# The two meta rows of a mixer output: matmuls replaced by elementwise products and a sum over partitions

## The chip, the cores and the metric

The kernel runs on one core of one Trainium2 chip. The metric is the device time of one execution, in microseconds (us); the time before is the median of three runs. Below, PE is TensorE, DVE is VectorE, ACT is ScalarE, POOL is GpSimd and SP is SyncE, whose queue issues nearly all DMA transfers.

## The reference

One layer of a hybrid decoder over 1024 tokens of 1024 channels, with 16 learned meta tokens ahead of them. Two mixers (a gated linear recurrence and a multi-scale pooling) give `z`, which is projected, normed and added to the residual; a gated MLP with a causal depthwise convolution of width 3 follows.

```python
z = sigmoid(gate_a) * (a @ w_branch_hgrn) + sigmoid(gate_b) * (p @ w_branch_pool)
h = h + rmsnorm(z @ w_out, mix_norm_post)
u = rmsnorm(h, ffn_norm_pre)
gt = causal_dwconv(u @ ffn_w_gate, ffn_conv_w, ffn_conv_b)      # 3 taps over time
y = (gelu(gt) * (u @ ffn_w_up)) @ ffn_w_down
h = h + rmsnorm(y, ffn_norm_post)
return h[:, N_META:]
```

The output drops the 16 meta tokens. The convolution looks two tokens back, so the MLP needs the residual of the last two meta tokens as well: two rows more than 1024. These two rows (the code calls them the halo, tile 8) are what the change is about: their part of `z @ w_out`.

## The kernel before, in words

All matrix products are done in float32 by splitting each operand into a high part (rounded to the format that TensorE multiplies at full rate, `F32R`) and a low part (the rest). A product then takes three matmuls: high by high, high by low, low by high (`mm3`, lines 245 to 248). High parts are made by casts on ACT, low parts by subtractions on DVE.

The stage around the change is the seam between the mixers and the MLP. `z` lies with its channels on the partitions, as 8 blocks `z[k]` of 128 channels by 1026 tokens; the first two token columns are the halo. `w_out` comes in 8 blocks of 128 channels by 1024 outputs (`wo` k). The 1024 rows are worked in three groups of row tiles of 128: tiles 0, 1, 2; then 3, 4, 5; then 6, 7. For group 0 the blocks k run upwards, for group 1 downwards, for group 2 upwards. A token `k.g.k.t` is one step: block k into tile t of group g, that is 6 matmuls of 512 columns (two halves of the outputs by three parts). Each tile accumulates in a pair of PSUM banks; there are four pairs.

The two halo rows are tile 8 of group 0. In step `k.0.k.8` their 2 columns of high and 2 columns of low z are the stationary operand, next to each other: 4 columns against the high weights and 2 against the low ones, for each half of the outputs, so 4 matmuls of 512 columns in each of the 8 steps (`mix_halo`, line 1453). That leaves high and low results in four rows; `part` copies them to SBUF and moves the low ones by a DMA to the first two partitions, and `join` adds them (lines 1494 to 1501).

Each `wo` k is read from `w_out` into one of three `wraw` buffers (line 1404), cast to `whi` (`wh.k`, line 1408), its rest put into `wlo` (`wl.k`, line 1412), three buffers each. `wl` also stores both parts to DRAM (`wos`, line 1414), because groups 1 and 2 need blocks again whose buffers are gone: `LOADS` says after which step which block is read back (line 1420), and into which buffers. `z[k]` is split for each group separately (`zh.g.k` on ACT, line 1329; `zl.g.k` on DVE, line 1333) into slots of a pool of 26 (`fm`).

When a tile is complete, its row work follows: `ga` (times a gain, line 1511) and `sq` (sum of squares on ACT, line 1506) read the PSUM pair and free it; `ad` adds the residual row (loaded by `res`) and stores the row; `qq`, `no` norm again; `tr` transposes 8 blocks on PE (line 1533); `up`, `lo` write high and low parts of the result as operands of the MLP. Rows 4 to 7 get further steps (`tk`, `su`, `di`, `b22`, `t1` to `t4`, `la`), which make the sums that a Strassen form of the MLP's first two matrices wants. Tokens `P1.e`, `P2.e` are the first products of that form; their weight parts were stored in DRAM earlier as `kept`, and the first of these need the `wraw` buffers.

The order of this stage is written out by hand: the string `SEAM` is a list of tokens, and each engine's instructions keep the order of the tokens (a manual schedule for PE, ACT, DVE and POOL). SP's order is not written out: the scheduler sets it from its own model of time. Waits are placed by the framework from data and buffers.

Of the kernel before, what the change touches and what calls it, by code (L numbers as in the profile page):

```python
# [14 lines left out]
P = 128  # L15
D = 1024
# [51 lines left out]
SEAM = ("k.0.0.0 wh.2 zh.0.4 wl.2 k.0.0.1 zh.0.5 zl.0.4 zh.0.6 k.0.0.2 zl.0.5 zh.0.7 zl.0.6 zh.1.7 k.0.0.8 zl.0.7 "  # L68
# [25 lines left out]
def trunk_kernel(ctx: ExitStack, tc: tile.TileContext, x, meta_tokens, mix_norm_pre,  # L94
# [1222 lines left out]
    def split_z(g, k):  # L1317
        at, n = HALO + GROUPS[g][0] * P, len(GROUPS[g]) * P
        if g == 2:
            if k % 2 == 0:  # L1320
                z_pairs[k // 2] = slot(4 * n, F32R, "zc")
            zc = z_pairs[k // 2][:, (k % 2) * 2 * n : (k % 2 + 1) * 2 * n]
        else:
            zc = slot(2 * n + (0 if g else 2 * HALO), F32R, "zc")
        cuts = [(zc[:, :n], zc[:, zc.shape[1] - n :], z[k][:, at : at + n])]
        if g == 0:
            cuts.append((zc[:, n : n + HALO], zc[:, n + HALO : n + 2 * HALO], z[k][:, :HALO]))
        for hi, _, src in cuts:
            act.copy(hi, src)

        def low():
            for hi, lo, src in cuts:
                dve.tensor_tensor(lo, src, rr(hi), ALU.subtract)

        return cuts[0][0], cuts[0][1], zc[:, n : n + 2 * HALO], low

    zt = ubig(F32, "z").rearrange("p (k t) -> p k t", k=KD)
    z0 = []
    def job_steps(kind, i):
        src, n_k, xs, chunks, post = job(kind, i)  # L1340
        if kind in ("BA", "BB"):
            load_gate(sas if kind == "BA" else sbs, kind == "BB", i)
            if kind == "BA" and i < EARLY_B:
                load_gate(sbs, True, i)
        ws = loader.next()
        if (kind, i) == ("BA", KD - 1):
            for k in range(ZA):
                z0.append(split_z(0, k))
                z0[k][3]()
        spare = [bank("spare") for _ in range(1 if (kind, i) == branch[-1] else 0)]  # L1350
        for b_ in spare:
            act.copy(b_[:, :1], eps_t)
        banks = [bank("p" + kind.lower()) for _ in chunks]
        for k, _ in enumerate(proj_steps(n_k, xs, chunks, ws, banks)):
            if k == 0:
                for b_ in spare:
                    act.copy(b_[:, 1:2], eps_t)
                loader.split()
            if k == n_k // 2 - 1:
                loader.low()  # L1360
                loader.load()
            yield
        if n_k == 1:
            loader.split()
            loader.low()
            loader.load()
        pay()
        after[kind, i] = post(banks)
        if kind == "BB" and i < EARLY_B:
            nc.sync.dma_start(sd[KD + i], sbs[i])  # L1370
        if kind == "BA":
            dve.tensor_tensor(sas[i], sas[i], sbs[i], ALU.add)
            z[i] = sas[i]
# [36 lines left out]
    def wo_low(k):  # L1410
        raw, hi, lo = wo[k]
        dve.tensor_tensor(lo, raw, rr(hi), ALU.subtract)
        for h, t in enumerate((hi, lo)):
            nc.sync.dma_start(wos[k][h], rr(t))
        wo[k] = hi, lo

    def wo_load(k, *tags):
        wo[k] = [slot(D, F32R, "wx") if t == "fm" else wst.tile([P, D], F32R, tag=t, name=nm(t)) for t in tags]
# [19 lines left out]
        z_at[g, k] = split_z(g, k)  # L1438

    def mix_tile(g, k, i, x_):  # L1440
        (whi, wlo), (zh, zl, _, _) = wo[k], z_at[g, k]
        t = slice(i * P, (i + 1) * P)
        ks = z_ks[g]
        for j in range(2):
            n = slice(j * 512, (j + 1) * 512)
            mm3(x_[:, n], (zh[:, t], zl[:, t]), (whi[:, n], wlo[:, n]), k == ks[0], k == ks[-1])

    def mix_halo(k, x_):
        (whi, wlo), (_, _, zm, _) = wo[k], z_at[0, k]
        for j in range(2):  # L1450
            n = slice(j * 512, (j + 1) * 512)
            for c, w in ((2 * HALO, whi), (HALO, wlo))[:: -1 if k else 1]:
                pe.matmul(x_[:c, n], zm[:, :c], w[:, n], start=(k == 0 and c > HALO), stop=(k == KD - 1),
                          skip_group_check=True)
# [21 lines left out]
    class Row:  # L1476
# [11 lines left out]
        def load(self):  # L1488
# [1 line left out]
            self.res = slot(D, name="row2")  # L1490
            nc.sync.dma_start(self.res[: self.n],
                              meta_tokens[T0:NM, :] if i == HALO_ROWS else x[0, i * P : (i + 1) * P, :])

        def part(self):
            both, self.low = slot(D, name="mhl"), slot(D, name="mlow")
            act.copy(both[: 2 * HALO], self.x[: 2 * HALO])
            nc.sync.dma_start(self.low[:HALO], both[HALO : 2 * HALO])
            self.x = both

        def join(self):  # L1500
            dve.tensor_tensor(self.x[:HALO], self.x[:HALO], self.low[:HALO], ALU.add)
# [55 lines left out]
        def last(self):  # L1557
            negdiff(dve, self.t2, self.t2, "b21", self.d)

    STEPS = dict(res=Row.load, part=Row.part, join=Row.join, sq=Row.square, ga=Row.gain, ad=Row.add, qq=Row.square2, no=Row.norm,  # L1560
                 tr=Row.turn, up=Row.up, lo=Row.low1, tk=Row.take, su=Row.sums, di=Row.diff, la=Row.last,
                 b22h=lambda r: upper("b22", r.c22, r.s), b22l=lambda r: lower("b22", r.c22, r.s),
                 t2h=lambda r: upper("t2", r.t2, r.d), t2l=lambda r: lower("t2", r.t2, r.d),
# [150 lines left out]
    for k in range(2):  # L1714
        wo_high(k)
        wo_low(k)
    ffn.lead, ffn.whole_pair = 3, True
    _, off, wide = ffn.span(0)
    x_ffn = {}
    LOADS = {(0, 7): ((4, "fm", "fm"),), (1, 7): ((3, "whi", "wlo"),), (1, 6): ((2, "whi", "wlo"),),  # L1720
             (1, 5): ((1, "whi", "wlo"),), (0, 6): ((0, "wraw", "wraw"),), (2, 0): ((5, "wraw", "wraw"),),
             (2, 1): ((6, "whi", "wlo"),), (2, 2): ((7, "whi", "wlo"),)}

    def seam(token):
        what, *arg = token.split(".")
        arg = [int(a) for a in arg]
        if what == "k":
            g, k, t = arg
            if t not in tiles_:
                tiles_[t] = pair("pm")  # L1730
            if t == HALO_ROWS:
                mix_halo(k, tiles_[t])
            else:
                mix_tile(g, k, t - GROUPS[g][0], tiles_[t])
            if t == (HALO_ROWS if g == 0 else GROUPS[g][-1]):
# [210 lines left out]
```

## Time and profile before

| | |
|---|---|
| median of 3 runs | 1315.32 us (1314.69 to 1315.69) |
| the profiled execution, its own time | 1315.41 us |
| its span, first to last instruction | 1313.4 us |
| mean granted TensorE clock | 0.996 |
| busy: PE, DVE, ACT, POOL | 1296.2, 920.3, 533.1, 362.7 us |
| group 0 of the mixer output, first matmul to the first of group 1 | 558.25 to 599.16 us |
| first matmul of the MLP products | 660.17 us |

A row of the timeline gives start, duration, engine, line of the kernel, operation, output and inputs, shape and count; in brackets the idle time before it and what ended it. A row of the groups gives line, engine, operation, names, shapes and count, then busy time in us and the mean of one in ns, then the idle time before. A row of waits gives who waited for whom: total us, times, the longest. The duration of a matmul in the timeline is from its start to its last result, longer than the distance to the next one.

### The profile page before, as it was taken

The page shows a single profiled execution, that of the slowest core. Times are in us where ns is not written, and L with a number is a line of the kernel's source. Part 1 is how long each engine was busy: PE and PEld are TensorE (multiplying, and loading weights), DVE is VectorE, ACT ScalarE, POOL GpSimd, SP SyncE. Part 2 cuts the span into 40 slices and gives each one's busy share as a digit, 9 for nine tenths or more (in the row PEclk, how much of TensorE's full clock was granted, in tenths as well). Part 3 has the DMA queues.
Part 4 walks back from the last instruction along what each step waited for, and adds up shares of the span by engine and source line. Part 5 has one row for each costly group of instructions (what it writes and reads, how often), then busy time and mean ns, then how long its engine had stood idle before and what let it go on. Part 6 is the DMA issues. An engine that isn't in the chain of part 4 may idle for free.

```text
span 1313.4 us, 19369 instructions
## 1 busy us (share of the span) xinstructions
PE 1296.2 (99%) x7385; PEld 1154.8 (88%) x7385; DVE 920.3 (70%) x1285; ACT 533.1 (41%) x946; POOL 362.7 (28%) x285
## 2 busy tenths in 40 slices
PE   8999999999999999999999999999999999999996
PEld 7799899999999999977898888888888888888884
DVE  6765777666867655556587888888778875556567
ACT  6553444444664633144462222223222232444443
POOL 5015332110006100000003555556565542001014
PEclk9999999999999999999999999999999999999998
DMA  7145876732111352496577777658866699666733
GB/s 276 58 144 154 266 260 206 252 93 65 35 51 37 124 214 81 160 340 222 208 255 239 204 208 208 183 163 208 205 161 170 177 253 257 226 226 215 262 125 126
DMA packets 143649, 240.31 MB, mean 183 GB/s; under 512 B 9406, under 2 KB 78626, under 8 KB 143558
## 3 DMA queue, kind: packets, MB, share of 16 engines
q1 hardware_dynamic: 132646, 218.90, 49.1%
q0 software_dynamic: 10912, 20.19, 10.2%
q8 instruction: 58, 0.95, 0.3%
q14 instruction: 33, 0.27, 0.1%
HBM read 168.20 MB, written 94.93 MB: 200 GB/s over the span
## 4 chain that ended last, share of the span: by engine, by line
PE 95%; DVE 2%; POOL 1%; DMA 1%; issue 1%; ACT 0%; SPq 0%; DVEq 0%; POOLq 0%; ACTq 0%
PE P L369 15%; PE P L366 15%; PE P L367 15%; PE pd L248 4%; PE pd L246 4%; PE pd L247 4%; PE pm L246 2%; PE pm L247 2%; PE pm L248 2%; PE sl L784 2%; PE pbb L256 1%; PE pba L256 1%; PE ppv L256 1%; PE pba L257 1%; PE pbb L257 1%; PE ppv L260 1%
## 5 line engine op out<-in xcount | busy, mean ns | idle before, releaser
L366 PE MATMUL P<-v,whi 128*128 128x512 f32 (+2 forms) x408 | 140.4, 352 | 0.0
L367 PE MATMUL P<-v,whi 128*128 128x512 f32 (+2 forms) x408 | 140.1, 351 | 0.0
L369 PE MATMUL P<-v,wlo 128*128 128x512 f32 (+2 forms) x424 | 135.2, 349 | 0.0
L248 PE MATMUL pd<-rot 128*128 128x512 f32 x272 | 105.9, 389 | 0.4 <-DVE rot L1694 0.4
L246 PE MATMUL pd<-rot 128*128 128x512 f32 x272 | 105.8, 389 | 0.0
L247 PE MATMUL pd<-rot 128*128 128x512 f32 x272 | 105.8, 389 | 0.0
L1607 POOL DMA_DIRECT2D wsum<-in_ffn_w_down_dram x22 | 18.7, 939 | 271.0 <-DMA wsum<-in_ffn_w_down_dram 271.0
L1694 DVE TENSOR_TENSOR rot<-wraw,rot 128x1024 fp32r<-128x1024 f32 x31 | 38.6, 1244 | 74.3 <-ACT rot L1693 74.3
L311 ACT CAST whi<-wraw 128x512 fp32r<-128x512 f32 x79 | 46.8, 619 | 104.8 <-PE P L367 81.0
L367 PEld LDWEIGHTS P<-v,whi 128*128 128x128 f32 x408 | 76.7, 188 | 10.2
L366 PEld LDWEIGHTS P<-v,whi 128*128 128x128 f32 x408 | 76.7, 188 | 10.0
L312 DVE TENSOR_TENSOR wlo<-wraw,whi 128x512 fp32r<-128x512 f32 x75 | 68.3, 929 | 23.1 <-ACT whi L311 23.1
L369 PEld LDWEIGHTS P<-v,wlo 128*128 128x128 f32 x424 | 74.1, 188 | 10.6
L337 POOL TENSOR_TENSOR swa<-wraw,wraw 128x512 f32<-128x512 f32 x29 | 47.5, 1639 | 107.2 <-DMA sscr<-sg 38.0
L1582 POOL TENSOR_TENSOR ys<-y 128x512 f32<-128x512 f32 x22 | 35.6, 1616 | 130.5 <-DVE y L1640 49.6
L1693 ACT CAST rot<-wraw 128x1024 fp32r<-128x1024 f32 x31 | 32.7, 1054 | 93.1 <-PE pd L248 91.7
L311 ACT CAST whi<-swa 128x512 fp32r<-128x512 f32 x58 | 34.5, 619 | 73.2 <-PE P L367 61.1
L1626 DVE SCALAR_TENSOR_TENSOR y<-g,par,y 128x1024 f32<-128x1024 f32 x44 | 63.5, 1444 | 0.8
L248 PEld LDWEIGHTS pd<-rot 128*128 128x128 f32 x272 | 51.1, 188 | 11.5 <-DVE rot L1694 0.8
L246 PEld LDWEIGHTS pd<-rot 128*128 128x128 f32 x272 | 51.1, 188 | 10.6
L311 ACT CAST whi<-swb 128x512 fp32r<-128x512 f32 x58 | 34.5, 618 | 63.8 <-PE P L367 59.6
L247 PEld LDWEIGHTS pd<-rot 128*128 128x128 f32 x272 | 51.1, 188 | 10.5
(421 smaller groups left out, 3978.7 us busy)
## 6 DMA issues: line engine op xcount, KB each, us to landing
wraw<-in_w_in_dram SPq DMA_DIRECT2D x36, 512.0 KB, 4.6
yt<-ysum SPq DMA_DIRECT2D x33, 512.0 KB, 4.4
wsum<-in_ffn_w_down_dram SPq DMA_DIRECT2D x22, 512.0 KB, 6.3
wraw<-in_ffn_w_gate_dram SPq DMA_DIRECT2D x20, 512.0 KB, 6.5
wraw<-in_ffn_w_up_dram SPq DMA_DIRECT2D x20, 512.0 KB, 4.1
ysum<-ys SPq DMA_DIRECT2D x11, 768.0 KB, 6.7
row<-in_x_dram SPq DMA_DIRECT2D x16, 512.0 KB, 6.3
wsum<-in_ffn_w_down_dram POOLq DMA_DIRECT2D x22, 256.0 KB, 7.3
```

Of the source, the lines that this page charges most:

```text
L246: pe.matmul(ps, ahi, bhi, start=first, stop=False)
L247: pe.matmul(ps, ahi, blo, start=False, stop=False)
L248: pe.matmul(ps, alo, bhi, start=False, stop=last)
L256: pe.matmul(ps[:, :n], whi[:, k, :], xhi, start=(k == 0), stop=False)
L311: act.copy(hi, src)
L312: (pool_e if 4 <= i < 2 * self.early else dve).tensor_tensor(lo, src, rr(hi), ALU.subtract)
L337: pool_e.tensor_tensor(s1, a21, a22, ALU.add)
L366: pe.matmul(d, whi[:, k, :], xh[:, c : c + w], start=(k == 0 and onto is None), stop=False, **go)
L367: pe.matmul(d, whi[:, k, :], xl[:, c : c + w], start=False, stop=False, **go)
L369: pe.matmul(x[:, o : o + w], wlo[:, k, :], xh[:, c : c + w], start=False, stop=(k == 3), **go)
L1626: dve.scalar_tensor_tensor(a, g[:, j : j + SEQ], cvw[:, j, m : m + 1], a, ALU.mult, ALU.add)
L1694: dve.tensor_tensor(lo, src, rr(hi), ALU.subtract)
```

## The change

The halo matmuls of the 8 steps go. Instead row t of the halo is made by `sum over k of wo_raw[k] * z[k][:, t]`, a 128 by 1024 product with one column of z as a scale for each partition, summed over k elementwise, and then summed over the 128 partitions by a matmul with columns of ones:

- `hp.k.t` makes a product on ACT (an activation `Copy` with the column as scale) and, if row t has a sum already, adds it there on POOL. Row 1 gets `hp.0.1` to `hp.7.1` in this way; row 0 gets only `hp.0.0`.
- `hv.k.0` adds block k to row 0 on DVE in one operation, for k from 1 to 7.
- `hh.t`, `hl.t` split the sum into high and low (slots of `fm`); `hl.0` also makes the ones.
- `hx`, after step `k.1.6.5`, is 8 matmuls: two halves of the outputs by two rows by high and low, with 2 columns as the stationary operand, of which one is ones. It takes its own PSUM pair then; before, tile 8 held one through group 0.

The products read `wraw` itself, so its buffer stays in use longer, and no parts of z for the halo are made. The sums lie in a new large tile `halo`, in a pool of two that the split inputs of earlier stages and the MLP operands share. `part` and `join` go, with their DMA. The loads `wr.k`, which stood at the end of a step of tile 8, and the stores `ws.k`, which stood in `wl`, are tokens of their own. Block 5 is read back into two slots of `fm` and no longer into two `wraw` buffers. All tokens of the stage are in a new order; beside the halo, splits of z for groups 1 and 2 stand later, `tr.5` stands ahead of `k.2.5.6`, and `tr.6` comes before `tr.7`.

```diff
-SEAM = ("k.0.0.0 wh.2 zh.0.4 wl.2 k.0.0.1 zh.0.5 zl.0.4 zh.0.6 k.0.0.2 zl.0.5 zh.0.7 zl.0.6 zh.1.7 k.0.0.8 zl.0.7 "
...
+SEAM = ("hp.0.0 hv.1.0 hp.0.1 hp.1.1 hp.2.1 hv.2.0 k.0.0.0 wh.2 wl.2 ws.2 k.0.0.1 wr.3 hv.3.0 zh.0.4 zl.0.4 zh.0.5 "
+        "hp.3.1 zl.0.5 k.0.0.2 k.0.1.0 wh.3 wr.4 wl.3 ws.3 zh.0.6 zl.0.6 k.0.1.1 k.0.1.2 wr.5 hv.4.0 hp.4.1 k.0.2.0 "
+        "wh.4 wl.4 ws.4 k.0.2.1 zh.1.6 wh.5 wl.5 zh.0.7 zl.0.7 zh.1.7 zl.1.7 k.0.2.2 k.0.3.0 hp.5.1 k.0.3.1 k.0.3.2 "
+        "k.0.4.0 wr.6 zh.1.5 wh.6 zh.1.4 wl.6 hp.6.1 hv.6.0 k.0.4.1 zl.1.4 hv.5.0 zl.1.6 wr.7 zh.1.3 k.0.4.2 k.0.5.0 "
+        "wh.7 wl.7 zh.1.0 k.0.5.1 res.1 k.0.5.2 k.0.6.0 res.0 hp.7.1 hv.7.0 zh.1.1 k.0.6.1 res.2 k.0.6.2 k.0.7.0 "
+        "k.0.7.1 zh.1.2 zl.1.2 ga.0 zh.2.2 sq.0 zl.1.5 ws.5 ws.6 ga.1 sq.1 k.0.7.2 ga.2 res.8 zl.1.0 ws.7 sq.2 ad.0 "
+        "ad.1 k.1.7.3 hh.1 hl.1 hh.0 hl.0 k.1.7.4 zh.2.3 ad.2 zh.2.0 zl.2.2 zl.2.0 zh.2.6 zh.2.1 zl.2.1 zl.1.1 zh.2.7 "
+        "k.1.7.5 zh.2.4 k.1.6.3 k.1.6.4 zh.2.5 k.1.6.5 hx ga.8 qq.0 no.0 qq.2 no.2 sq.8 qq.1 k.1.5.3 no.1 k.1.5.4 "
+        "k.1.5.5 tr.0 up.0 lo.0 zl.1.3 ad.8 zl.2.6 k.1.4.3 k.1.4.4 tr.1 zl.2.7 up.1 lo.1 k.1.4.5 k.1.3.3 k.1.3.4 tr.2 "
...
+        "tr.4 tk.4 ahead.4 k.2.4.6 k.2.4.7 res.6 b22h.4 tr.5 su.4 k.2.5.6 k.2.6.6 k.2.7.6 tk.5 di.4 t2h.4 t1h.4 t2l.4 "
+        "t1l.4 res.7 k.2.5.7 sq.6 b22h.5 su.5 ga.6 ad.6 b22l.4 t3h.4 k.2.6.7 k.2.7.7 sq.7 ga.7 P1.0 qq.6 t2h.5 t1h.5 "
...
+halo_parts = ubig(F32, "halo").rearrange("p (i c) -> p i c", i=KD)
...
-    def mix_halo(k, x_):
-        (whi, wlo), (_, _, zm, _) = wo[k], z_at[0, k]
-        for j in range(2):
-            n = slice(j * 512, (j + 1) * 512)
-            for c, w in ((2 * HALO, whi), (HALO, wlo))[:: -1 if k else 1]:
-                pe.matmul(x_[:c, n], zm[:, :c], w[:, n], start=(k == 0 and c > HALO), stop=(k == KD - 1),
-                          skip_group_check=True)
+    def halo_product(k, t):
+        to = halo_parts[:, HALO + next(turns) % (KD - HALO) if t in halo else t, :D]
+        act.activation(to, wo_raws[k], AF.Copy, scale=z[k][:, t : t + 1])
+        if t in halo:
+            pool_e.tensor_tensor(halo[t], halo[t], to, ALU.add)
+        else:
+            halo[t] = to
+
+    def halo_more(k, t):
+        dve.scalar_tensor_tensor(halo[t], wo_raws[k], z[k][:, t : t + 1], halo[t], ALU.mult, ALU.add)
+
+    def halo_high(t):
+        halo[t, 0] = slot(D, F32R, "hhi")
+        act.copy(halo[t, 0], halo[t])
+
+    def halo_low(t):
+        halo[t, 1] = slot(D, F32R, "hlo")
+        dve.tensor_tensor(halo[t, 1], halo[t], rr(halo[t, 0]), ALU.subtract)
+
+        if t == 0:
+            rows1 = small([P, HALO * HALO], "rows1", "qm", 2)
+            dve.memset(rows1, 0.0)
+            dve.memset(rows1[:, :: HALO + 1], 1.0)
+            halo["rows"] = rows1.bitcast(F32R)
+
+    def halo_sum():
+        x_ = tiles_[HALO_ROWS] = pair("pm")
+        for j in range(2):
+            n = slice(j * 512, (j + 1) * 512)
+            for i in range(2 * HALO):
+                t = i // 2
+                pe.matmul(x_[:HALO, n], halo["rows"][:, t * HALO : (t + 1) * HALO], halo[t, i % 2][:, n],
+                          start=i == 0, stop=i == 2 * HALO - 1)
...
-             (1, 5): ((1, "whi", "wlo"),), (0, 6): ((0, "wraw", "wraw"),), (2, 0): ((5, "wraw", "wraw"),),
+             (1, 5): ((1, "whi", "wlo"),), (0, 6): ((0, "wraw", "wraw"),), (2, 0): ((5, "fm", "fm"),),
```

More of the change, by code (lines that the diff above doesn't have):

```diff
@@ L1323, in split_z @@
         else:
[L1324 to L1329, printed above, removed]
+            zc = slot(2 * n, F32R, "zc")
+        hi, lo, src = zc[:, :n], zc[:, n:], z[k][:, at : at + n]
+        act.copy(hi, src)
         def low():
-            for hi, lo, src in cuts:
-                dve.tensor_tensor(lo, src, rr(hi), ALU.subtract)
-        return cuts[0][0], cuts[0][1], zc[:, n : n + 2 * HALO], low
+            dve.tensor_tensor(lo, src, rr(hi), ALU.subtract)
+        return hi, lo, low
     zt = ubig(F32, "z").rearrange("p (k t) -> p k t", k=KD)
@@ L1348, in job_steps @@
                 z0.append(split_z(0, k))
-                z0[k][3]()
+                z0[k][2]()
         spare = [bank("spare") for _ in range(1 if (kind, i) == branch[-1] else 0)]
@@ L1399, in trunk_kernel @@
     wos = [dram.tile([2, P, D], F32, name=f"wos{k}") for k in range(KD)]
-    wo = {}
+    wo, wo_raws = {}, {}
     def wo_raw(k):
-        wo[k] = wraw_tile()
+        wo[k] = wo_raws[k] = wraw_tile()
         nc.sync.dma_start(wo[k], w_out[0][k * P : (k + 1) * P])
@@ L1412, in wo_low, with wo_store @@
         dve.tensor_tensor(lo, raw, rr(hi), ALU.subtract)
-        for h, t in enumerate((hi, lo)):
+        wo[k] = hi, lo
+    def wo_store(k):
+        for h, t in enumerate(wo[k]):
             nc.sync.dma_start(wos[k][h], rr(t))
-        wo[k] = hi, lo
     def wo_load(k, *tags):
@@ L1440, in mix_tile @@
     def mix_tile(g, k, i, x_):
-        (whi, wlo), (zh, zl, _, _) = wo[k], z_at[g, k]
+        (whi, wlo), (zh, zl, _) = wo[k], z_at[g, k]
         t = slice(i * P, (i + 1) * P)
@@ L1446, in mix_tile @@
             mm3(x_[:, n], (zh[:, t], zl[:, t]), (whi[:, n], wlo[:, n]), k == ks[0], k == ks[-1])
-    def mix_halo(k, x_):
-        (whi, wlo), (_, _, zm, _) = wo[k], z_at[0, k]
+    halo = {}
+    turns = iter(range(2 * KD))
+    def halo_product(k, t):
[20 more added lines that the diff above has]
+        x_ = tiles_[HALO_ROWS] = pair("pm")
         for j in range(2):
             n = slice(j * 512, (j + 1) * 512)
-            for c, w in ((2 * HALO, whi), (HALO, wlo))[:: -1 if k else 1]:
-                pe.matmul(x_[:c, n], zm[:, :c], w[:, n], start=(k == 0 and c > HALO), stop=(k == KD - 1),
-                          skip_group_check=True)
+            for i in range(2 * HALO):
+                t = i // 2
+                pe.matmul(x_[:HALO, n], halo["rows"][:, t * HALO : (t + 1) * HALO], halo[t, i % 2][:, n],
+                          start=i == 0, stop=i == 2 * HALO - 1)
     z_ks = [list(range(KD)), list(range(KD))[::-1], list(range(KD))]
@@ L1492, in load @@
                               meta_tokens[T0:NM, :] if i == HALO_ROWS else x[0, i * P : (i + 1) * P, :])
[L1494 to L1501, printed above, removed]
         def square(self):
@@ L1558, in last @@
             negdiff(dve, self.t2, self.t2, "b21", self.d)
-    STEPS = dict(res=Row.load, part=Row.part, join=Row.join, sq=Row.square, ga=Row.gain, ad=Row.add, qq=Row.square2, no=Row.norm,
+    STEPS = dict(res=Row.load, sq=Row.square, ga=Row.gain, ad=Row.add, qq=Row.square2, no=Row.norm,
                  tr=Row.turn, up=Row.up, lo=Row.low1, tk=Row.take, su=Row.sums, di=Row.diff, la=Row.last,
@@ L1716, in trunk_kernel @@
         wo_low(k)
+        wo_store(k)
     ffn.lead, ffn.whole_pair = 3, True
@@ L1730, in seam @@
                 tiles_[t] = pair("pm")
[L1731 to L1735, printed above, removed]
+            mix_tile(g, k, t - GROUPS[g][0], tiles_[t])
+            if t == GROUPS[g][-1]:
                 for load in LOADS.get((g, k), ()):
                     wo_load(*load)
-                if g == 0 and k + 3 < KD:
-                    wo_raw(k + 3)
         elif what == "wh":
@@ L1743, in seam @@
             wo_low(*arg)
+        elif what == "hp":
+            halo_product(*arg)
+        elif what == "hv":
+            halo_more(*arg)
+        elif what == "hh":
+            halo_high(*arg)
+        elif what == "hl":
+            halo_low(*arg)
+        elif what == "hx":
+            halo_sum()
+        elif what == "wr":
+            wo_raw(*arg)
+        elif what == "ws":
+            wo_store(*arg)
         elif what == "zh":
@@ L1746, in seam @@
         elif what == "zl":
-            z_at[tuple(arg)][3]()
+            z_at[tuple(arg)][2]()
         elif what == "quarters":
```

23 rows, old and new, of the table SEAM are left out of this document.

## The prediction

> **What bounds the kernel now.** I read the page first: the profiled execution took 1315.41 us with a span of 1313.4 us, and TensorE holds both the busy time and the chain that ends last.
>
> ```profile
> span 1313.4 us, 19369 instructions
> PE 1296.2 (99%) x7385; PEld 1154.8 (88%) x7385; DVE 920.3 (70%) x1285; ACT 533.1 (41%) x946; POOL 362.7 (28%) x285
> PE 95%; DVE 2%; POOL 1%; DMA 1%; issue 1%; ACT 0%; SPq 0%; DVEq 0%; POOLq 0%; ACTq 0%
> ```
>
> The change lies in the mixer output stage, so next come the windows of that stage: the end of the branch products, the three groups of rows, and the first gate products (columns: window; its length; busy PE, weight loads, DVE, ACT, POOL; clock; DMA share; GB/s).
>
> ```profile
> 540.00:558.20 18.20, 18.20 (x116) 18.20 (x115) 11.01 (x22) 3.21 (x10) 0.00 (x0) 1.00 0.63 218
> 558.20:599.30 41.10, 41.10 (x179) 29.85 (x178) 21.52 (x38) 16.27 (x33) 0.00 (x0) 1.00 0.80 294
> 599.30:626.90 27.60, 27.60 (x134) 22.43 (x133) 17.48 (x25) 13.79 (x30) 0.00 (x0) 1.00 0.63 229
> 626.90:660.00 33.10, 33.10 (x164) 27.69 (x165) 21.28 (x36) 16.83 (x42) 0.00 (x0) 1.00 0.59 218
> 660.00:700.00 40.00, 39.41 (x309) 38.15 (x308) 31.26 (x59) 22.31 (x49) 0.00 (x0) 1.00 0.70 245
> ```
>
> TensorE is never idle from 540 to 660 us, at full clock; VectorE and ScalarE have 40 to 60% to spare and GpSimd does nothing at all. So a matmul taken out here shortens the end by its own slot, unless something that had slack takes its place. TensorE's own waits from 655 us to the end are two, and the first is in reach of this diff:
>
> ```profile
> PE P L369 <- DMA wraw<-kept0l: 0.6, 1, 0.6
> PE pd L248 <- DVE rot L1694: 0.4, 1, 0.4
> 657.42 0.33 SPq L301 DMA_DIRECT2D wraw<-kept0l  x1
> 661.40 0.51 PE L369 MATMUL P<-v,wraw 128*128 128x258 f32 x2 [0.59 <-DMA wraw<-kept0l]
> ```
>
> **The change, part by part.** *Removed from TensorE.* The two meta rows cost four matmuls in each of the 8 steps of group 0, 32 in all. They are 2 or 4 columns wide on the weight side, but stream all 512 columns, and the timeline shows what that costs:
>
> ```profile
> 558.25 0.40 PE L246 MATMUL pm<-whi,zc 128*128 128x512 f32 x1
> 562.44 0.39 PE L1453 MATMUL pm<-whi,zc 128*4 128x512 f32 x1
> 562.67 0.40 PE L1453 MATMUL pm<-wlo,zc 128*2 128x512 f32 x1
> 562.90 0.39 PE L1453 MATMUL pm<-whi,zc 128*4 128x512 f32 x1
> 563.13 0.40 PE L1453 MATMUL pm<-wlo,zc 128*2 128x512 f32 x1
> 563.37 0.40 PE L246 MATMUL pm<-whi,zc 128*128 128x512 f32 x1
> 599.16 0.40 PE L246 MATMUL pm<-whi,zc 128*128 128x512 f32 x1
> ```
>
> From 558.25 to 599.16 there are 8 x (18 + 4) = 176 matmuls, so one slot is 40.91 / 176 = 0.2324 us, and the narrow ones take the same slot. The change puts 8 back (columns of ones, also 512 columns streamed; the 2-column rows above are their price). Net 24 x 0.2324 = 5.58 us. That is the main term.
>
> *The stall at 661.40.* It stands because wo 5 is reloaded into the wraw buffers, which the first kept operand also wants; kept0l is issued only at 657.42, when wo 5's last step is through. The diff moves wo 5 into two fm slots. wo 0 then leaves wraw after step k.2.0.7, some 20 us earlier (632 in the new count of slots), so I take the 0.59 us as gained (bounds: 0 if another load holds it up, 0.59).
>
> *Added off TensorE.* Nearest rows, the first two and the fourth from the whole run:
>
> ```profile
> L1515 DVE SCALAR_TENSOR_TENSOR m<-m,rstd,row 128x1024 f32<-128x1024 f32 x8 | 10.3, 1285 | 0.3
> L1011 ACT ACTIVATE phi<-ppp,par 128x342 fp32r<-128x342 f32 x12 | 5.7, 550 | 1.6 <-PE ppp L260 1.6
> L1408 ACT CAST whi<-wraw 128x1024 fp32r<-128x1024 f32 x6 | 6.3, 1050 | 18.1 <-PE pba L257 6.8 <-PE pm L1453 5.2 <-DMA wos<-whi 4.1
> L184 POOL TENSOR_TENSOR wlo<-wraw,whi 128x1024 fp32r<-128x1024 f32 x5 | 13.0, 2602 | 39.3 <-ACT whi L182 26.7 <-DMA vh<-vscr 12.6
> L1412 DVE TENSOR_TENSOR wlo<-wraw,whi 128x1024 fp32r<-128x1024 f32 x6 | 7.3, 1223 | 9.9 <-ACT whi L1408 9.9
> L1333 DVE TENSOR_TENSOR zc<-z,zc 128x384 fp32r<-128x384 f32 x12 | 6.1, 553 | 0.0
> L1511 DVE TENSOR_TENSOR m<-pm,g 128x1024 f32<-128x1024 f32 x3 | 3.7, 1225 | 9.7 <-PE pm L248 9.7
> ```
>
> ScalarE gets nine products of 128x1024 (hp), between 1.05 us each (the cast of that size) and 3 x 0.55 = 1.65 us (the activation with a column as scale, three times its width): 9.5 to 14.9 us; I take 1.05, the row of the same size. VectorE gets seven hv at 1.285 = 9.0 us. GpSimd gets seven additions at 2.60 = 18.2 us. Then two hh (2.1 us) and two hl (2.4 us), ahead of the sum hx. Gone are part, join, the 2-column splits and a store that waited for part.
>
> Do they stay beside TensorE? Group 0 is now 144 slots, 558.25 to 591.7. The last hp stands after k.0.6.0 (about 584.9), so row 1 is summed by some 589. hx stands after k.1.6.5: 36 more slots, 600.1. VectorE up to 588.9, when the first tile ends and ga.0 can start: hv 9.0, six wl 7.3, eight zl 4.4, the end of the last branch product 2.6 (its z rows of 1.35 and 1.22 us), together 23.3 us of the 31.7 from its last earlier work at 557.2:
>
> ```profile
> 554.93 2.24 DVE L1333 TENSOR_TENSOR zc<-z,zc 128x384 fp32r<-128x384 f32 x8
> 558.13 1.35 DVE L1046 TENSOR_TENSOR z<-z,pba 128x342 f32<-128x342 f32 x3 [0.96 <-PE pba L260]
> 561.01 1.22 DVE L1372 TENSOR_TENSOR z<-z,sa 128x1026 f32<-128x1026 f32 x1
> ```
>
> After that, in its queue: three ga 3.7, two zl 1.1, two ad 2.9, two hl and the ones 2.6, together 10.3 us, so hl.0 ends at 599.2, 0.9 us ahead of hx. ScalarE is looser: 16.3 us of its 41 were used, and four hp can fall into the 6.8 us that it waited for TensorE before wh.2. I cost all of it at nothing. If that cover is gone, whatever hl.0 is late goes onto TensorE one for one, since everything of steps k.1.5 to tr.0 queues behind hx.
>
> *Moved: loads, stores, buffers.* The wraw buffer of wo k is now also read by hp and hv, so wr.3 to wr.7 are issued later (wr.3 after hp.0.1, near 553). What a load takes, and that the queue of SP issues by readiness and not by place (these rows stand behind k.0.6.0 in the order, at 586, and were issued at 567):
>
> ```profile
> DMA to landing us min/median/max: 4.7/6.4/8.0
> 566.95 1.25 SPq L1491 DMA_DIRECT2D row<-in_x_dram  x2
> ```
>
> The first is wraw's. Against 4.7 to 8.0 us, wh.3 isn't due before k.0.3 at 570.8, less 2.3 us for wh and wl; all later ones have the same 8 us or more. The stores of wo 5 to 7 stand behind ga and sq, beside the reloads. The pairs of PSUM no longer hold row 8 through group 0, so k.1.7.3 finds one free; hx takes the pair that tile 2 leaves, and tr.0 the one that ga.8 and sq.8 leave, 4.2 us after hx for some 2.5 us of work. I cost these at nothing too.
>
> Sum: 1315.41 - 5.58 - 0.59 = 1309.24 us. The profiled execution stood 0.09 us over the median of the runs (1315.32), so 1309.2 us.
>
> **The rivals.** *A: GpSimd slows VectorE.* This stage had no GpSimd work. Elsewhere the two collide:
>
> ```profile
> 394.65 2.38 DVE L845 TENSOR_TENSOR dks<-qf,kk 128x512 f32<-128x512 f32 x1
> 397.72 0.69 DVE L847 TENSOR_TENSOR nk<-dks,nk 128x512 fp32r<-128x512 f32 x1 [0.69 <-ACT nk L846]
> 393.73 2.76 POOL L973 TENSOR_TENSOR s<-s 128x1027 f32<-128x1027 f32 x1
> L312 DVE TENSOR_TENSOR wlo<-wraw,whi x75: 677/687/1780, 69.5 to 1075.3; 128x512 fp32r<-128x512 f32 x75
> ```
>
> A 0.69 us operation of two tensors took 2.38 us under one GpSimd addition, 3.4 times as long. Seven additions of up to 2.76 us are 19.3 us in which VectorE loses up to 71%, 13.7 us, if it always has work; it has work 23.3 / 31.7 of the time, so 10.1 us, against 8.4 us of slack. VectorE would then reach ga.0 1.7 us late, and wl.7 or hl.0 would hold TensorE for 1 to 2 us: 1310.2 to 1311.2. Against it: additions come one at a time behind hp, and VectorE waits for wh between them. (The Trainium skill's GPSIMD Engine Reference, section "Key points", says that GpSimd shares its SBUF interfaces with VectorE and contends with VectorE instructions that have two SBUF inputs; hv and wl are of this kind, and the rows at 394 agree.)
>
> *B: the reloads bind.* Six stores of wo 5 to 7, two loads of wo 4 and three stores of finished rows are 11 x 0.524 = 5.8 MB from about 590 us, and wo 4 is due for k.1.4.3 at 606.9. At the 294 GB/s of group 0 they take 19.7 us, and TensorE would wait 2.8 us: 1312.0. At the rate of a full window they take 14.1 us and nobody waits:
>
> ```profile
> 610.00:620.00 10.00, 10.00 (x50) 8.35 (x49) 6.95 (x10) 3.83 (x8) 0.00 (x0) 1.00 1.02 410
> ```
>
> For it: these stores now stand late. Against: the queue of SP need not keep them waiting for that place.
>
> *C: slots (the slower side).* wo 5 now needs two of the 26 fm slots at about 633 us, when by the code 24 are held: g2, g3; eight of t2 and t4; wo 4's two; four of z; three each of res and un, two of m1; 24 + 2 = 26. The pool is already short near here, as SP's waits for row loads show:
>
> ```profile
> SPq L1491 <- DVE un L1526: 2.0, 1, 2.0
> SPq L1491 <- PE pt L1533: 1.6, 1, 1.6
> ```
>
> If the slots only come free with tr.5, just ahead of k.2.5.6 (646.7), the load lands 6.4 us late (the median above), and wo 6 and wo 7, queued behind it on SP, add about 2 us: 1309.2 + 8.4 = 1317.6. It decides from 6.2 us of stall on. Against: ad.3 frees a slot early.
>
> *D: the change doesn't do what it says.* Were the narrow matmuls free on TensorE, or the stage bound elsewhere, nothing would move: 1315.3. The slots above speak against it.
>
> **How the numbers follow.** Forecast as summed, give or take 0.8 us: 62%. A and B together 20%; each alone stays below 1312.7 us, both at once don't (1309.2 + 2.0 + 2.8 = 1314.0), so three quarters of it count as faster. C 9%. D, or B and C in a size that just eats the gain: 9%. A measurement of this kernel can tell about 0.2%, 2.6 us, from no change. Faster: 0.62 + 0.15 = 0.77; same: 0.05 + 0.07 = 0.12; slower: 0.09 + 0.02 = 0.11. The range starts where the slots are 0.2324 us and some small stall goes as well, 1308.3, and goes up through A and B and part of both at once to 1313.0; C and D are what is left out.
>
> **What would show it.** Right: 24 matmuls fewer at 512 columns, group 0 some 33.5 us long, no wait of TensorE on hl, wl or wo before the gate products, kept0l issued near 633 us, GpSimd busy 13 to 20 us there. Wrong in A: hv or wl of 2 us and more, and TensorE waiting for wlo or hlo. Wrong in B or C: a wait on DMA at L246 to L248 for wx, whi or wlo, or hscr and wos queued on SP behind wx. The forecast fails altogether if TensorE idles over 6 us more than before anywhere after 558 us.

## The result and the profile after

The changed kernel takes 1308.62 us (median of six runs, 1308.06 to 1308.93). The kernel before took 1315.12 us on the same chip (median of six, 1314.69 to 1315.69). The ratio is 0.995 with a 95% interval of 0.9937 to 0.9962, so it is faster by 6.5 us, or 0.5%. The forecast was 1309.2 us. The profiled execution of the changed kernel took 1308.07 us, 7.34 us less than that of the kernel before (1315.41).

From the page of the changed kernel, the span, the busy times and the chain by engine:

```profile
span 1305.8 us, 19342 instructions
PE 1288.7 (99%) x7361; PEld 1152.2 (88%) x7361; DVE 941.7 (72%) x1287; ACT 542.4 (42%) x948; POOL 382.2 (29%) x292
PE 92%; DMA 2%; DVE 2%; POOL 1%; issue 1%; ACT 1%; SPq 0%; DVEq 0%; POOLq 0%; ACTq 0%
```

TensorE has 24 matmuls fewer (7361 against 7385) and 7.5 us less of busy time, and it still sets the end. The other three engines do 50.2 us more between them (21.4, 9.3 and 19.5).

The windows of the stage, with the columns of the prediction; the second row is the new group 0:

```profile
540.00:558.10 18.10, 18.10 (x115) 18.10 (x115) 15.80 (x20) 5.02 (x9) 6.09 (x2) 1.00 0.62 215
558.10:591.54 33.44, 33.44 (x150) 27.56 (x149) 31.52 (x28) 18.52 (x27) 14.24 (x5) 1.00 0.81 300
591.54:618.00 26.46, 26.46 (x130) 21.11 (x129) 21.87 (x37) 17.33 (x38) 0.00 (x0) 1.00 0.83 317
618.00:653.40 35.40, 35.40 (x174) 29.39 (x173) 24.00 (x41) 16.78 (x42) 0.00 (x0) 1.00 0.63 225
653.40:693.00 39.60, 39.60 (x310) 38.46 (x310) 30.29 (x57) 22.29 (x49) 0.00 (x0) 1.00 0.68 235
```

TensorE has no idle time in any of them. In group 0 VectorE went from 21.52 of 41.10 us to 31.52 of 33.44.

Where the time went shows in TensorE's timeline. First the kernel before, in the rows that the prediction did not need (start, duration, engine, line, operation):

```profile
600.32 0.39 PE L248 MATMUL pm<-whi,zc 128*128 128x512 f32 x1
600.68 0.50 PE L246 MATMUL pm<-whi,zc 128*128 128x512 f32 x1
601.01 0.39 PE L247 MATMUL pm<-wlo,zc 128*128 128x512 f32 x1
...
604.26 0.39 PE L246 MATMUL pm<-whi,zc 128*128 128x512 f32 x1
...
606.98 0.39 PE L246 MATMUL pm<-whi,zc 128*128 128x512 f32 x1
...
660.17 0.28 PE L366 MATMUL P<-v,wraw 128*128 128x258 f32 x1
...
660.54 0.28 PE L367 MATMUL P<-v,wraw 128*128 128x256 f32 x1
...
691.19 0.28 PE L366 MATMUL P<-t2h,whi 128*128 128x258 f32 x1
```

Then the changed kernel:

```profile
558.12 0.40 PE L247 MATMUL pm<-whi,zc 128*128 128x512 f32 x1
...
561.60 0.39 PE L247 MATMUL pm<-whi,zc 128*128 128x512 f32 x1
...
590.61 0.39 PE L249 MATMUL pm<-whi,zc 128*128 128x512 f32 x1
...
653.44 0.28 PE L367 MATMUL P<-v,wraw 128*128 128x258 f32 x1
...
653.92 0.40 PE L370 MATMUL P<-v,wraw 128*128 128x258 f32 x2
...
683.59 0.28 PE L367 MATMUL P<-t2h,whi 128*128 128x258 f32 x1
```

From the first mixer matmul to the first gate product (called "the stage" from here on) it was 660.17 - 558.25 = 101.92 us and is 653.44 - 558.12 = 95.32 us: 6.60 us less. From there to the first product of `t2h` it was 691.19 - 660.17 = 31.02 us and is 30.15: the stall on kept0l is gone, worth 0.87 us and not the 0.59 that its row named (the start ahead of it, 660.54, is 0.86 us earlier, where the products otherwise follow at 0.12; and the pair that waited took 0.51 us, where it takes 0.40 at 653.92). Together 7.47 us, against 7.34 for the whole execution.

The 6.60 us hold more than the 24 slots at 0.2324 us (5.58). The matmuls of 512 columns run at two paces. From 604.26 to 606.98 the kernel before ran 12 in 2.72 us, 0.2267 us each; its whole group 0 went at 0.2324. In the changed kernel group 0 goes at 0.2267 from 561.60 on: 128 slots to 590.61 make 29.01 us. The mean over group 0 went from 0.2325 to 0.2272 us, which on its 144 matmuls is 0.76 us. Both paces stand at a granted clock of 1.00.

A gap is gone as well. In the kernel before, the two slots from 600.32 to 601.01 take 0.69 us in place of 0.46, and the changed kernel has nothing like it: 0.23 us. The trace names no wait there, so its cause stays open; the three edited versions of the kernel before, below, all have it.

### The profile page after: what moved, and what is told of

The parts are those of the page before. It is cut to its first block, busy times and chain, and to the rows that moved or that the text cites. A ratio compares the mean times of both kernels' runs of the same rounds, so it can differ in the third digit from the quotient of the medians.

```text
span 1305.8 us, 19342 instructions
## 1 busy us (share of the span) xinstructions
PE 1288.7 (99%) x7361; PEld 1152.2 (88%) x7361; DVE 941.7 (72%) x1287; ACT 542.4 (42%) x948; POOL 382.2 (29%) x292
## 4 chain that ended last, share of the span: by engine, by line
PE 92%; DMA 2%; DVE 2%; POOL 1%; issue 1%; ACT 1%; SPq 0%; DVEq 0%; POOLq 0%; ACTq 0%
PE P L367 14%; PE P L370 14%; PE P L368 14%; PE pd L249 4%; PE pd L247 4%; PE pd L248 4%; PE pm L247 2%; PE pm L249 2%; PE pm L248 2%; PE sl L785 2%; PE pbb L257 1%; PE pba L257 1%; PE ppv L257 1%; PE pba L258 1%; PE pbb L258 1%
## 5 line engine op out<-in xcount | busy, mean ns | idle before, releaser
L367 PE MATMUL P<-t4h,whi 128*128 128x258 f32 (+1 forms) x204 | 59.1, 306 | 0.0
```

The costliest lines, as they stand in the source:

```text
L367: pe.matmul(d, whi[:, k, :], xh[:, c : c + w], start=(k == 0 and onto is None), stop=False, **go)
```

## The experiments

In these comparisons the kernel before was run on the same chip each time, so the ratios can be compared and the times of different chips cannot. Stage lengths come from the timeline as above.

**The removed slots, and which pace the rest keeps.** The kernel before without the narrow matmuls in six of its eight steps, and with them made 128 columns wide:

```diff
 def mix_halo(k, x_):
     ...
+    if 0 < k < KD - 1:
+        return
```

> The kernel before without the 24 narrow halo matmuls of steps k = 1 to 6 (the two meta rows then get only blocks 0 and 7 of their sum; nothing else changes). Theory of slots alone: 24 x 0.2324 = 5.58 us less, 1309.5, and the other matmuls of group 0 stay 0.2324 us apart. Theory that a narrow matmul also slows those behind it: from some 20 matmuls behind step 0's narrow ones up to step 7's the spacing is 0.2267, about 111 matmuls x 0.0057 = 0.63 us more, 1308.9.

Measured: 1311.07 us, ratio 0.996 (0.9947 to 0.9974). The stage in its timeline:

```profile
559.51 0.40 PE L246 MATMUL pm<-whi,zc 128*128 128x512 f32 x1
...
655.79 0.28 PE L366 MATMUL P<-v,wraw 128*128 128x258 f32 x1
```

96.28 us, 5.64 less than before, against 24 x 0.2324 = 5.58. This shows the main term by itself, in the old order. The rest of group 0 stayed at 0.232 us with no narrow matmul for six steps, so narrow neighbours are not what slows it. The first gate products behind the stage took 30.57 us here, 0.45 less than in the kernel before: part of the stall on kept0l goes when the slots go, without any edit to its buffer.

```diff
-pe.matmul(x_[:c, n], zm[:, :c], w[:, n], ...)
+pe.matmul(x_[:, n], z_at[0, k][0][:, :P], w[:, n], ...)
```

> The kernel before with the same count of halo matmuls, but each with a stationary operand of 128 columns (the block's first 128 high columns of z in place of the 2 or 4 halo columns), so the two meta rows hold other sums. If the width of the stationary operand is what slows the matmuls behind it: spacing 0.2267 through group 0, 196 x 0.0057 = 1.1 us less, 1314.0. If it is their count, their turn to a fourth PSUM pair or anything else in the order: 0.2324 as before and 1315.1.

Measured: 1315.58 us, ratio 0.9994 (0.9985 to 1.0003), stage 101.35 us. As many matmuls as before, and 0.57 us less: part of group 0 ran at the quick pace, from 575 us on. That is neither what the one theory said nor the other.

**One matmul more in each step.** The changed kernel with an unused matmul in each of the 8 steps of group 0, once with 2 columns as the stationary operand, once with 128, into a PSUM pair of its own:

```diff
+if g == 0 and t == 2:
+    if k == 0:
+        extra.append(pair("px"))
+    pe.matmul(extra[0][:HALO, :512], z_at[0, k][0][:, :HALO], wo[k][0][:, :512], start=True, stop=True)
```

> The changed kernel with one more matmul at the end of each of group 0's 8 steps, 2 columns of z as the stationary operand, 512 streamed, into the free PSUM pair and read by nobody. Theory that a narrow matmul slows those behind it: spacing 0.2324 through group 0 as in the kernel before, so the stage is 8 x 0.2324 + 144 x 0.0057 = 2.7 us longer than 95.3. Theory that it costs its slot alone: 1.9 us longer, spacing 0.2267.

> The same with 128 columns as the stationary operand of the extra matmul. If the width matters: spacing 0.2267 and the stage 8 x 0.2267 = 1.8 us longer. If any extra matmul into another pair slows the rest: 0.2324 and 2.7 us longer, as with 2 columns.

One run each: stages of 100.60 and 100.52 us, 5.2 to 5.3 us more than the changed kernel where 8 slots are 1.9. I had not foreseen that the extra pair waits for a memset that stands late in VectorE's order (TensorE's waits of the first; the second has the same row):

```profile
PE px L1757 <- DVE first L1380: 3.2, 1, 3.2
```

Without those 3.2 us, 2.0 to 2.1 are left for 8 slots. What the two runs still say is in their difference: 2 columns and 128 cost the same within 0.08 us. Of the pace they say a little more: behind the stall, 130 slots of group 0 took 29.62 us in the first run (566.85 to 596.47) and 29.48 in the second (566.77 to 596.25), 0.2278 and 0.2268 each. The six narrow ones among them did not bring 0.2324 back; whether the stall ahead of them has a part in that is not shown.

**The move of wo 5 alone**, in the kernel before:

```diff
-(2, 0): ((5, "wraw", "wraw"),),
+(2, 0): ((5, "fm", "fm"),),
```

> The kernel before with one word changed: block 5 of w_out is read back into two fm slots and not into wraw. If the stall ahead of the MLP products hung on the wraw buffer, TensorE's wait on kept0l goes (0.59 us idle, 0.86 us from the last matmul before it to the next) and the time falls by 0.6 to 0.9 us, to 1314.2 to 1314.5. If another load or a shortage of slots takes its place: within 0.2 us of 1315.1, or slower.

Measured: 1316.64 us, ratio 1.0001 (0.9993 to 1.001). The stall on kept0l went, and the gate products took 30.16 us as in the changed kernel, but the stage grew to 103.14, by 1.22. SP's issues and TensorE's timeline show where:

```profile
641.50 0.38 SPq L301 DMA_DIRECT2D wraw<-kept1h  x1
...
646.98 0.68 SPq L1420 DMA_DIRECT2D whi<-wos  x1
```

```profile
657.64 0.50 PE L246 MATMUL pm<-whi,zc 128*128 128x512 f32 x1 [0.94 <-DMA whi<-wos]
```

The kept operands now go out early, ahead of the reloads of the mixer weights wo 6 and wo 7. The matmul that waited is the first of `k.2.7.6`, and the high weights of wo 7 came 0.94 us late for it. The wait moved from one load to another. That the kept loads held up this one is read from the order and from full DMA engines (share 0.99 to 1.03 from 640 us on); no run tests it. In the changed kernel the same edit comes with another order, in which neither waits. SP's issues there, with the loads of wo 5 at 625.08 (at 639.69 in the run above), well ahead of the kept operands:

```profile
583.84 0.64 SPq L1415 DMA_DIRECT2D wos<-whi  x1
586.48 0.32 SPq L1415 DMA_DIRECT2D wos<-wlo  x1
...
588.12 1.30 SPq L1420 DMA_DIRECT2D wx<-wos  x2
...
625.08 4.40 SPq L1420 DMA_DIRECT2D wx<-wos  x2
...
631.65 0.32 SPq L302 DMA_DIRECT2D wraw<-kept0l  x1
```

The reverse, the changed kernel with wo 5 back in wraw, has no run, so what the new order has of the gain and what the buffer has is not shown.

**What the products and additions cost.** The changed kernel without them (row 0 keeps one product and row 1 one):

```diff
 def halo_product(k, t):
+    if t in halo:
+        return
...
 def halo_more(k, t):
+    return
```

> The changed kernel without the products and additions of blocks 1 to 7 (hp and hv beyond block 0 left out: the two meta rows then miss these blocks). If the added work on ScalarE, GpSimd and VectorE costs nothing, as forecast: 1308.6, within 0.3 us. If the collisions of GpSimd and VectorE cost something that the stage hides elsewhere: 0.5 us and more below.

Measured: 1309.17 us, ratio 0.9949 (0.9936 to 0.9961); stage 95.27 us against 95.32. They cost the end nothing. Its window of group 0 shows what they cost VectorE:

```profile
560.69:594.10 33.41, 33.41 (x150) 27.55 (x149) 16.75 (x23) 13.25 (x22) 0.00 (x0) 1.00 0.93 344
```

Without them VectorE is busy for 16.75 us, with them for 31.52, a difference of 14.8. The five `hv` in this window at 1.28 us make 6.4. The other 8.4 us are the same operations taking longer, the z rows above all and the `hv` themselves, as the groups of the changed kernel on VectorE in group 0 show (the last but one number is the mean in ns):

```profile
L1330 DVE TENSOR_TENSOR zc<-z,zc 128x384 fp32r<-128x384 f32 x9 | 11.5, 1282 | 0.0
L1461 DVE SCALAR_TENSOR_TENSOR halo<-wraw,z,halo 128x1024 f32<-128x1024 f32 x5 | 8.6, 1721 | 0.0
```

The z rows took 0.553 us before and take 1.28; the `hv` take 1.72, and 1.281 in a run below without GpSimd. In the timeline of the changed kernel, on GpSimd and on VectorE:

```profile
560.92 3.03 POOL L1456 TENSOR_TENSOR halo<-halo 128x1024 f32<-128x1024 f32 x1 [9.23 <-ACT halo L1454]
...
561.61 2.76 DVE L1330 TENSOR_TENSOR zc<-z,zc 128x384 fp32r<-128x384 f32 x1
...
577.47 3.51 DVE L1461 SCALAR_TENSOR_TENSOR halo<-wraw,z,halo 128x1024 f32<-128x1024 f32 x1
577.49 2.39 POOL L1456 TENSOR_TENSOR halo<-halo 128x1024 f32<-128x1024 f32 x1 [1.03 <-ACT halo L1454]
...
581.37 1.27 DVE L1461 SCALAR_TENSOR_TENSOR halo<-wraw,z,halo 128x1024 f32<-128x1024 f32 x1
581.46 3.44 POOL L1456 TENSOR_TENSOR halo<-halo 128x1024 f32<-128x1024 f32 x1 [1.57 <-ACT halo L1454]
...
582.56 2.75 DVE L1330 TENSOR_TENSOR zc<-z,zc 128x384 fp32r<-128x384 f32 x1
...
588.32 1.23 DVE L1532 TENSOR_TENSOR m<-pm,g 128x1024 f32<-128x1024 f32 x1 [0.20 <-PE pm L249]
...
595.92 2.36 DVE L1469 TENSOR_TENSOR hlo<-halo,hhi 128x1024 fp32r<-128x1024 f32 x2 [0.39 <-ACT hhi L1465]
```

One z row of 0.55 us lasted 2.76 under an addition. The rows read as waiting rather than as a slower pace. A z row that starts under an addition ends 0.42 us after it (564.37 behind 563.95) or 0.41 (585.31 behind 584.90), and the `hv` that starts with an addition at 577.47 ends 1.10 us after it (580.98 behind 579.88), nearly its whole 1.28. In the same way the addition that starts under an `hv` at 581.46 ends 2.26 us after that (584.90 behind 582.64). In these rows the two engines take turns. So an addition of some 2.3 us costs a VectorE that has work more than the `hv` of 1.28 us that it replaces.

VectorE came to `ga.0` (588.32) with 0.20 us to spare, and hl.0 ended at 598.28, 0.74 us ahead of the first matmul of `hx` at 599.02.

The new operations on GpSimd, in the groups of the changed kernel (the nine products on ScalarE take 1.146 us each):

```profile
L1456 POOL TENSOR_TENSOR halo<-halo 128x1024 f32<-128x1024 f32 x7 | 20.3, 2905 | 129.9 <-ACT halo L1454 129.9
```

Then the sum of row 1 without GpSimd and ScalarE, all on VectorE:

```diff
 def halo_product(k, t):
-    to = halo_parts[:, HALO + next(turns) % (KD - HALO) if t in halo else t, :D]
+    if t in halo:
+        return halo_more(k, t)
+    to = halo_parts[:, t, :D]
     ...
```

> The changed kernel with row 1 summed like row 0, by VectorE alone (hp of blocks 1 to 7 becomes one VectorE operation of 1.28 us; no GpSimd work, less ScalarE work, no collisions). In group 0 VectorE was busy 31.5 of 33.4 us, of which some 6 us were lost to collisions. Five more operations are 6.4 us in that window: about the same load. Theory that work on GpSimd saves VectorE nearly nothing here: 1308.6, within 0.4 us. Theory that GpSimd carries what VectorE has no room for: TensorE waits for wlo, 1309.5 and more.

Measured: 1310.22 us, ratio 0.9953 (0.9941 to 0.9966); stage 95.29 us. Its window of group 0, and two of its groups there:

```profile
561.06:594.50 33.44, 33.44 (x150) 27.57 (x149) 28.35 (x33) 13.29 (x22) 0.00 (x0) 1.00 0.93 339
```

```profile
L1463 DVE SCALAR_TENSOR_TENSOR halo<-wraw,z,halo 128x1024 f32<-128x1024 f32 x10 | 12.6, 1281 | 0.0
L1330 DVE TENSOR_TENSOR zc<-z,zc 128x384 fp32r<-128x384 f32 x9 | 4.9, 552 | 0.0
```

With twice the `hv` VectorE is busy 28.35 us, which is less than the 31.52 of the kernel in which GpSimd takes that row from it. The z rows are back at 0.552 us. ScalarE's products of row 1 are gone here too; that the lost time is GpSimd's doing shows in the next run, where GpSimd's work alone grows.

**The cover taken away.** GpSimd's additions doubled:

```diff
     pool_e.tensor_tensor(halo[t], halo[t], to, ALU.add)
+    pool_e.tensor_tensor(to, to, to, ALU.add)
```

> The changed kernel with each of the seven GpSimd additions followed by a second one whose result nobody uses. The first additions were 2.4 to 3.4 us and VectorE ended its queue ahead of ga.0 with 0.2 us to spare. If that spare time is all there is (theory A: GpSimd's time costs VectorE's time, one for one where they meet): VectorE falls behind by several us, TensorE waits for wlo or for hlo for 2 to 6 us, 1310.6 to 1314.6. If the queues take it up elsewhere: 1308.6.

Measured: 1320.65 us, ratio 1.0027 (1.0016 to 1.0038): slower than the kernel before, and the stage is 106.02 us, 10.7 more than in the changed kernel. The added group on GpSimd, TensorE's waits in the stage, and two windows of it:

```profile
L1457 POOL TENSOR_TENSOR halo<-halo 128x1024 f32<-128x1024 f32 x7 | 18.6, 2663 | 0.5
```

```profile
PE pm L248 <- DVE wlo L1410: 6.8, 4, 3.9
```

```profile
560.85:594.40 33.55, 29.84 (x129) 23.34 (x127) 33.55 (x22) 16.53 (x24) 26.42 (x10) 1.00 0.57 204
598.60:602.40 3.80, 3.75 (x10) 2.93 (x11) 3.14 (x4) 0.23 (x1) 0.00 (x0) 0.55 0.98 289
```

18.6 us more on GpSimd leave VectorE no idle time in the first window, most of group 0, and TensorE waits four times for `wl`, the low weights that VectorE makes, and once for z: 7.6 us together. Behind the longest wait (3.9 us, up to 598.65) TensorE also runs slower. Its granted clock falls to 0.55, and nine slots take 3.73 us, to 602.38, where they took 2.04 at the quick pace: 1.7 us more. The remaining 1.4 us have no row; as at kept0l, a gap between starts is longer than the idle time shown for it. I had expected 2 to 6 us: the direction was right and the size was not.

Then `hl` held up by two unused operations of VectorE:

```diff
 def halo_low(t):
     ...
+    if t == 1:
+        for _ in range(2):
+            dve.tensor_tensor(halo_parts[:, 2, :D], halo[t], halo[t], ALU.add)
```

> The changed kernel with two more VectorE additions of 128x1024 (2.3 us, result unused) just ahead of hl.1. hlo was ready 0.7 us before hx began. Forecast's theory, that lateness of hl goes onto TensorE one for one: a wait of TensorE on hlo of 1.6 us, 1310.2. If matmuls or the queue behind take it up: 1308.6.

Measured: 1310.63 us, ratio 0.9955 (0.9941 to 0.9968); stage 96.77 us, 1.45 more. Its timeline on VectorE and TensorE:

```profile
596.67 2.48 DVE L1471 TENSOR_TENSOR halo<-halo 128x1024 f32<-128x1024 f32 x2
...
599.06 2.35 DVE L1472 TENSOR_TENSOR hlo<-halo,hhi 128x1024 fp32r<-128x1024 f32 x2
...
601.70 0.40 PE L1486 MATMUL pm<-hhi,rows 128*2 128x512 f32 x1 [1.29 <-DVE rstd L1498]
```

Counted from the start of the stage (559.35 here, 558.12 in the changed kernel), hl.0 ended 1.90 us later: 42.06 us in, and not 40.16. That is less than the added 2.48, since part of it fell into the 0.39 us that VectorE waited ahead of `hl` anyway. The first matmul of `hx` started 0.29 us after the end of hl.0, because it also needs the ones, whose memsets follow hl.0 (the wait is put down to `rstd`, which stands between them). So the 0.74 us of the changed kernel were 0.45 us of slack, and 1.90 less 0.45 is 1.45: what is late there passes to the end one for one.

**The places of the stores.** The changed kernel with its `ws` stores back in `wl`:

```diff
 elif what == "wl":
     wo_low(*arg)
+    wo_store(*arg)
...
 elif what == "ws":
-    wo_store(*arg)
+    pass
```

> The changed kernel with each block's two stores put back behind its split (wl), in place of their own places in the order. If the stores' places matter (rival B: the reloads bind): TensorE waits on a reload, whi or wx from wos, 0.5 us and more. If SP's queue issues by readiness anyway: within 0.3 us of the changed kernel.

Measured: 1308.97 us, ratio 0.9947 (0.9933 to 0.996); stage 95.33 us. The places of the stores are worth nothing that can be seen. In the changed kernel the last of them were issued at 583.84 and 586.48 (SP's rows above), ahead of `ga.0` at 588.32, behind which `ws.5` to `ws.7` are written: in SP's order, which is the scheduler's and not the string's, they stood further forward already.

**The pace.** In group 0 of the kernel before, the low part of each z tile stands four columns further on, behind the columns of the meta rows. The changed kernel with that place again:

```diff
-zc = slot(2 * n, F32R, "zc")
-hi, lo, src = zc[:, :n], zc[:, n:], z[k][:, at : at + n]
+zc = slot(2 * n + (0 if g else 2 * HALO), F32R, "zc")
+hi, lo, src = zc[:, :n], zc[:, zc.shape[1] - n :], z[k][:, at : at + n]
```

> The changed kernel with one thing of the kernel before: in group 0 the low part of each z tile stands four columns (16 bytes) further on, as it did when the tile also held the columns of the meta rows. Nothing else differs, and the result is the same. It asks whether the place of the stationary operands sets the pace of the matmuls in group 0, which was 0.2324 us in the kernel before, also with the narrow matmuls left out, and 0.2267 us in the changed kernel. If the place sets it, the mean spacing goes from 0.2277 to about 0.2295 us, the stage from the first mixer matmul to the first gate product from 95.3 to about 96.0 to 96.3 us, and the time goes up by 0.7 to 0.9 us. If it does not, the spacing stays at 0.2275 to 0.2279 us and the stage at 95.3 us. Against the place speaks the run with wide halo matmuls, which had the old place and the quick pace from 575 us on. I give the place 35%.

Its timeline:

```profile
557.71 0.40 PE L247 MATMUL pm<-whi,zc 128*128 128x512 f32 x1
...
574.65 0.39 PE L248 MATMUL pm<-wlo,zc 128*128 128x512 f32 x1
...
576.98 0.39 PE L249 MATMUL pm<-whi,zc 128*128 128x512 f32 x1
...
653.74 0.28 PE L367 MATMUL P<-v,wraw 128*128 128x258 f32 x1
```

From 574.65 to 576.98 are 10 slots of 0.233 us, where the changed kernel had 0.2267. The stage is 653.74 - 557.71 = 96.03 us, 0.71 more; the mean of group 0 is 0.2322 us. So the place of the low z parts alone brought the slow pace back to group 0. This rests on one trace of that kernel, against nine that have the new place (the changed kernel, its second run and seven edited versions): from about its 16th matmul on, group 0 runs at 0.227 to 0.229 us in all nine, outside of waits and the matmuls right behind them. The time (1308.39 us, ratio 0.9953, 0.9937 to 0.997) cannot tell 0.7 us. The place isn't the whole rule: the run with wide halo matmuls had the old place and the quick pace from 575 us on, and in other groups slow stretches stand too (the changed kernel runs `hx` at 0.232, and the first 6 to 9 full slots behind a transposition at 0.231 or so).

**The changed kernel once more, on another chip:**

> The changed kernel itself, beside the kernel before on one chip with more rounds. Between the first matmul of the mixer output and the first product P6, the two traces so far differ by 7.47 us (101.92 + 31.02 against 95.32 + 30.15), the medians by 6.5. If the trace's difference is what the change is worth: 7.2 to 7.6 us below the kernel before. If some of it is lost elsewhere in most executions: 6.3 to 6.8 below.

Measured: 1308.64 us against 1315.76, ratio 0.9944 (0.9931 to 0.9958), 7.1 us; stage 95.30 us, the first gate products 30.15. The stage comes back to 0.02 us. The 7.1 lie between the two expectations, nearer to the first.

## Why the prediction was right, and where its steps were off

- *The narrow matmuls, 5.58 us.* Right: leaving out 24 of them in the old order gave 5.64 us. A matmul with 2 columns costs its slot like one with 128 (0.08 us between the two over 8 slots). Rival D is out.
- *The stall on kept0l, 0.59 us.* The mechanism held: kept0l was issued at 631.65 (forecast: near 632) and nothing waited. The size was off: 0.87 us, since the idle time in the row is not the whole gap between starts, and the pair that had waited was longer as well. The step also took the gain for one of the buffer alone. By itself the edit is worth nothing (ratio 1.0001): in the old order the 0.9 us reappear as a wait for wo 7. And leaving out narrow matmuls took 0.45 us off the same products without the edit. The gain was seen with the edit and the new order together.
- *Missing from the sum: the pace of the other matmuls, 0.76 us.* The step that failed is the one that counted group 0 as 144 slots of 0.2324. It took the old pace for granted, though 0.2267 stood in the same trace behind 604.26. The new layout of the z tiles, which the prediction did not weigh at all, accounts for 0.71 of it.
- The sum so mended, with the gap at 600.32 that the prediction did not see (0.23), is 5.58 + 0.87 + 0.76 + 0.23 = 7.44 of the 7.47 us seen. Outside this stretch 0.13 us went the other way (7.47 to 7.34). The forecast gain was 6.17 us, so it was 1.2 us short of the trace. That the median came out within 0.6 us of the forecast is partly luck: the medians differ by 6.5 us in the first comparison and by 7.1 in the second.
- *Added work at nothing.* Right for the end (stage 95.27 without it, 95.32 with it), with far less to spare than stated. VectorE's slack ahead of `ga.0` was put at 8.4 us, with seven `hv` counted; two of them ran ahead of group 0, so the same sum with five gives 11.0. In the trace VectorE idled 1.92 us in all of group 0, and 0.20 ahead of `ga.0`. hl.0 was put at 599.2 with 0.9 us to spare, and ended at 598.28 with 0.74, of which 0.45 were slack. So the cover held by less than half a microsecond, which the prediction did not foresee: that it held is in part luck. The products on ScalarE took 1.15 us (forecast 1.05), the additions on GpSimd 2.905 (forecast 2.60).
- *Rival A.* Its collision happened: VectorE lost 8.4 us in group 0 to it (bound: up to 10.1). Of its two signs one came, an `hv` of over 2 us (3.51 at 577.47), and the other didn't: TensorE waited for nothing. It was the nearest rival; doubling GpSimd's work made it real, with 10.7 us. (The Trainium skill's GPSIMD Engine Reference, section "Key points", names this contention with VectorE instructions of two SBUF inputs; the traces agree, with 0.55 us turned into 2.76, and 1.28 on the mean.)
- *hl one for one.* Right: 1.45 us for 1.90 of lateness less 0.45 of slack.
- *Rival B.* Absent, and its premise did not hold: the last store was issued at 586.48 and did not stand late. The loads of wo 4 were issued at 588.12, and no matmul waited for a transfer. The prediction read from two row loads that SP's queue issues by readiness; what those rows show is that its order is not that of the string.
- *Rival C.* Absent. The slots for wo 5 came free at about 625 us, when its loads were issued.

## What to carry to other kernels

Where TensorE sets the end, a matmul with few stationary columns costs what a full one costs per streamed column, and moving such work to idle engines pays by the slot; count the slots, and look in the same trace for the pace that the remaining ones could have. Work that is "free" on idle engines can use up their slack by slowing each other: VectorE and GpSimd have to be costed here as taking turns, at the durations seen when they overlap, and the same result came without GpSimd at all. Freeing a load's buffer only helps if the loads that then stand behind it are not due sooner. A slack read off one row is too large where the waiting instruction needs something else as well.

## What the runs showed of the hardware

- Matmuls of 512 float32 columns in the rounded format run at 0.2324 or at 0.2267 us, at the same granted clock of 1.00. Moving the low half of the stationary operands by four columns (16 bytes) switched a whole group from the one to the other (0.2272 to 0.2322 us on the mean, one trace). Why, and what else switches it, stays open.
- One GpSimd addition of 128x1024 stretched a VectorE subtraction of 128x384 from 0.55 to 2.76 us; 14.24 us of them in group 0 took 8.4 us from VectorE. Operations that began under an addition ended 0.41, 0.42 and 1.10 us after it, so in these rows the two took turns. Once VectorE's slack was gone, 18.6 us more on GpSimd cost the end 10.7 us.
- Behind a wait of 3.9 us TensorE ran nine slots at 0.41 us on the mean, at a granted clock of 0.55 (window 598.60 to 602.40). Behind the wait of 3.2 us in the run with one narrow matmul more, the granted clock was 1.00 (window 566.40 to 570.00).
